# One layer on one Trainium2 core: where the first up weights are cast, and two buffers shared by three kinds of small tile

## The chip, the cores and the metric

The kernel runs on one core of one Trainium2 chip. Its time is device microseconds for one launch, from a comparison of several executions; lower is better. A core has a matrix engine (TensorE, PE in the profile, with its weight loads as PEld), VectorE (DVE), ScalarE (ACT), GpSimd (POOL), and SyncE (SP), which here issues nearly all DMA transfers. Each engine works through its own instructions strictly in order and waits on semaphores for the others.

## The reference, cut to what matters

One decoder layer over a sequence of 1024 rows and a width of 1024, all in float32:

```python
xn = rmsnorm(x, attn_norm_g)
proj = einsum('bsd,de->bse', xn, w_in)            # q, k, v of both head groups, forget gates
out_a = swa_sinks_attention(qa, ka, va, sinks)    # 8 heads, window of 128, ALiBi
out_b = forgetting_attention(qb, kb, vb, log_f)   # 8 heads, causal, bias c[t] - c[s]
x = x + einsum('bse,ed->bsd', concat(out_a, out_b), w_out)
hn = rmsnorm(x, mlp_norm_g)
hid = square(relu(einsum('bsd,df->bsf', hn, w_up)))     # 4096 wide
x = x + einsum('bsf,fd->bsd', hid, w_down)
```

q and k are normalised per head; `c` is the running sum of the logarithms of the forget gates.

## The kernel before, in words

**Split operands.** To keep float32 accuracy every matmul operand is split into a rounded part hi and a remainder lo = x - hi, and three products are summed (hi·hi, hi·lo, lo·hi). The helper `split` (L75) does this for weights: line L77 is the cast on ACT that writes hi, line L80 the subtraction, on POOL or DVE, that writes lo. So one pair of weights is one ACT cast, then one subtraction, and TensorE needs both. For the activations `h_split` (L975) does the same with the gain of the norm folded in: L977 is the cast on ACT, L978 the remainder on DVE.

**Order of the work.** The code is traced as it stands; the framework then orders the instructions of each engine by a simulated timeline, with priorities that follow the traced order. `tc.high_priority` lifts a block in it, and `with tc.issue_after(ins):` forces every instruction traced in the block that runs on the engine of `ins` to be issued after `ins`. The order on each engine is fixed at build time. Buffers are named by tags: tiles of one tag take turns in its `bufs` places, and the first writer of a new tile waits until the last user of the place is done.

**Attention.** TensorE projects q, k, v for a pair of heads (`proj`) while the heads before are scored. In the forgetting heads (`scores_b`, L672) a block of 128 queries is scored against up to 1024 keys in pieces of 512 columns (`spb`). For the piece on the diagonal POOL first copies the broadcast decay row with the future masked out (`cm`, L694), then one DVE instruction adds it to the scores and takes the row minimum (L699), ACT takes the exponential (L704), and for the last pair of heads DVE or POOL normalises (L711, L713, L715). TensorE transposes the probabilities (`tpb`, L740), ACT and DVE split them (`pth` L402, `ptl` L403), and TensorE multiplies by v (`pvb`). The norms of q and k (`qknorm`, L266) square a block on POOL into a tile `sq` (L279) that DVE then sums (L284). The gates (`forget_gates`, L466) work in a tile `zt`. Before the change `sq` and `zt` share one place of 512 columns, and `cm` has one place of its own, of the same size.

**Output projection.** `w_out` is taken in 8 columns blocks `dt`, the first four row tiles of each during attention (`out_first`, the sums go to memory as `part_d`), the other four at the end: dt = 0 and 4 beside the last attention units, then dt = 1, 5, 2, 6, 3, 7. `out_weights` (L869) loads and splits the weights into a place given by the list `WOS`. `out_finish` (L982) loads `part_d` into `h` (place w2 for dt < 4, w3 for 4 to 6, a tile `rr` for dt = 7), adds the sums of TensorE (L988), stores h to memory (`h_d`, L989), and splits h for the next stage. For dt < 4 this is `h_split` of the left half (product 1), and the cast `b12` (L994) of the right half into place w4; for dt > 3 it is `h_split` of both halves (products 2 and 3) and three DVE sums `ts` (L1007), which are split as well (`sum_splits`, products 5, 6, 7 and 4).

**Up projection.** The 4096 columns are made 2 x 128 at a time (index j of 16) by seven products, a Strassen-Winograd scheme, in the order `UP = (1, 2, 3, 6, 7, 5, 4)`. One product is 12 matmuls over four row tiles k: hi·hi, hi·lo, lo·hi for each k. The split activations `bh[n]`, `bl[n]` stay in place for all j; the row tile k = 3 of each comes from dt = 3 and dt = 7, the last to be finished. `up_weights` (L1048) takes the next of seven weight places from `w_slot` (L1044) and splits; lo is written by DVE for n in (2, 6, 5) and by POOL for 1, 3, 7, 4. For j = 0 and j = 1 the weights of product 1 are split ahead (`up_ahead`), and TensorE runs product 1 for both before product 2. The weight places w0 to w6 are shared with `h`, `b12` and the weights of the output projection, which is why their rotation matters here.

**Down projection.** Seven products again, in four phases; the page's lines `pd`, `hx` and `wx` belong to it. The change does not touch it.

Of the kernel before, what the change touches and what calls it, by code (L numbers as in the profile page):

```python
# [8 lines left out]
F32 = mybir.dt.float32  # L9
# [7 lines left out]
P = 128  # L17
# [38 lines left out]
def hybrid_layer(  # L56
# [209 lines left out]
    def qknorm(x, nh, tlo, thi, r=None):  # L266


        n = thi - tlo
        w = nh * HD  # L270
        ss, r0, u = (
            ap3.tile([P, 16], F32, tag=tag, name=tag, bufs=2)[:, : n * nh]
            for tag in ("ss", "sr0", "su")
        )
        m = n // 2
        for i in range(2):
            sq = ap2.tile([P, 512], F32, tag="sq", name="sq", bufs=1)[:, : m * w]
            xv = x[:, tlo + i * m : tlo + (i + 1) * m, :w]
            square = nc.gpsimd.tensor_tensor(  # L279
                out=sq.rearrange("p (t c) -> p t c", t=m), in0=xv, in1=xv, op=ALU.mult  # L280
            )
            if i == 0:
                squared.append(square.ins)
            nc.vector.tensor_reduce(  # L284
                out=ss[:, i * m * nh : (i + 1) * m * nh],
                in_=sq.rearrange("p (g d) -> p g d", d=HD), axis=AX.X, op=ALU.add,
            )
        th = lambda a: a.rearrange("p (t h) -> p t h", h=nh)
        nc.vector.scalar_tensor_tensor(
            out=th(ss), in0=th(ss), scalar=1.0 / HD,  # L290
            in1=ep2[:, tlo:thi].unsqueeze(2).to_broadcast([P, n, nh]),
            op0=ALU.mult, op1=ALU.add,
        )
        nc.scalar.activation(r0, ss, AF.Ln)
        nc.scalar.activation(r0, r0, AF.Exp, scale=-0.5)
        nc.vector.tensor_tensor(out=u, in0=r0, in1=r0, op=ALU.mult)
        nc.vector.tensor_tensor(out=u, in0=u, in1=ss, op=ALU.mult)
        na = nh + (2 if r is not None else 0)
        if r is None:
            rv = ap3.tile([P, 16], F32, tag="r", name="r", bufs=2)[:, : n * nh]  # L300
            rv = th(rv)
        else:
            rv = r[:, tlo:thi, :]
        nc.vector.scalar_tensor_tensor(
            out=rv[:, :, :nh], in0=th(u), scalar=3.0, in1=th(r0),
            op0=ALU.subtract, op1=ALU.mult,
        )
        for t in range(n):
            xt = x[:, tlo + t, : na * HD].rearrange("p (h d) -> p h d", d=HD)
            nc.gpsimd.tensor_tensor(  # L310
                out=xt, in0=xt, in1=rv[:, t].unsqueeze(2).to_broadcast([P, na, HD]), op=ALU.mult
            )
# [153 lines left out]
    def forget_gates():  # L466
        nc.vector.tensor_tensor(
            out=z, in0=z, in1=bfb.unsqueeze(2).to_broadcast([P, NH, NT]), op=ALU.add
        )
        zf = z.rearrange("p h t -> p (h t)")  # L470

        zt = ap2.tile([P, 4, NT * NH], F32, tag="sq", name="zt", bufs=1)
        ze, zs, zp = zt[:, 0], zt[:, 1], zt[:, 2]
        nc.vector.scalar_tensor_tensor(out=ze, in0=zf, scalar=-1.0, in1=zf, op0=ALU.mult, op1=ALU.min)
        nc.scalar.activation(ze, ze, AF.Exp)
        nc.vector.tensor_scalar(out=zs, in0=ze, scalar1=2.0, scalar2=None, op0=ALU.add)
        nc.vector.reciprocal(zs, zs)
        nc.vector.tensor_tensor(out=zs, in0=zs, in1=ze, op=ALU.mult)
        nc.vector.tensor_tensor(out=ze, in0=zs, in1=zs, op=ALU.mult)
        nc.vector.tensor_scalar_mul(zp, ze, 2.0 / 17.0)  # L480
        for n in (15, 13, 11, 9, 7, 5, 3):
            nc.vector.scalar_tensor_tensor(
                out=zp, in0=zp, scalar=2.0 / n, in1=ze, op0=ALU.add, op1=ALU.mult
            )
        nc.vector.scalar_tensor_tensor(out=zp, in0=zp, scalar=2.0, in1=zs, op0=ALU.add, op1=ALU.mult)
        nc.vector.scalar_tensor_tensor(
            out=zt[:, 3], in0=zf, scalar=0.0, in1=zp,
            op0=ALU.min, op1=ALU.subtract,
        )
        pt = pa.tile([P, 512], F32, tag="tr", name="ptf", bufs=3)  # L490
        nc.tensor.transpose(pt[: NH * NT, :P], zt[:, 3], ident)
        cum = ap2.tile([P, 256], F32, tag="mt", name="cum", bufs=2)[: NH * NT, :P]
        nc.vector.tensor_tensor_scan(
            out=cum, data0=ones1[: NH * NT].to_broadcast([NH * NT, P]),
            data1=pt[: NH * NT, :P], initial=0.0, op0=ALU.mult, op1=ALU.add,
        )
        off = pa.tile([P, 512], F32, tag="tr", name="off", bufs=3)
        mm(
            off[: NH * NT, 0:1], before.rearrange("p h t -> p (h t)"),
            cum[:, P - 1 : P], True, True,  # L500
        )
        offs = ap3.tile([NH * NT, 1], F32, name="offs")
        nc.vector.tensor_copy(offs, off[: NH * NT, 0:1])
        nc.vector.tensor_scalar(
            out=cum, in0=cum, scalar1=offs[:, 0:1], scalar2=None, op0=ALU.add
        )
        nc.sync.dma_start(c_d.rearrange("h (t q) -> (h t) q", q=P), cum)
# [164 lines left out]
    def scores_b(p, qp, h):  # L672
        q1, k1, k2, cb = heads[p, "q"][h], heads[p, "k1", h], k2_of[h], heads[p, "cb", h]
        probs = []
        for i in (2 * qp, 2 * qp + 1):
# [8 lines left out]
            for c in range((nk + 511) // 512):  # L684
                n = min(512, nk - c * 512)
                ne = max(n, 256)
                ks = slice(c * 512, c * 512 + ne)
                sp = pa.tile([P, 512], F32, tag="sc", name="spb", bufs=2)
                mm(sp[:, :ne], qs, k1[:, ks], True, False)
                pe = mm(sp[:, :ne], qs, k2[:, ks], False, True)  # L690
                bias = cb[:, c * 512 : c * 512 + n]
                if (c + 1) * 512 >= nk:
                    cm = ap2.tile([P, 512], F32, tag="cm", name="cm", bufs=1)[:, :n]
                    nc.gpsimd.affine_select(  # L694
                        out=cm, in_=bias, pattern=[[-1, n]], compare_op=ALU.is_ge,
                        fill=BIG, base=n - P, channel_multiplier=1,
                    )
                    bias = cm
                nc.vector.tensor_tensor_reduce(  # L699
                    out=pr[:, c * 512 : c * 512 + n], in0=sp[:, :n], in1=bias, scale=1.0,  # L700
                    scalar=3e38 if c == 0 else nm[:, 0:1],
                    op0=ALU.add, op1=ALU.min, accum_out=nm[:, c : c + 1],
                )
# [159 lines left out]
        mix_tiles(e)  # L863
        return nc.sync.dma_start(mixt[e].bitcast(F32), mixs_d[e].rearrange("c p s -> p c s"))

    WOS = ("w5", "w6", "w0", "w1", "w5", "w6")
    nout = [0]

    def out_weights(dt, e0):  # L869
        i = nout[0] = nout[0] + 1  # L870
        wr = o["zw"].tile([P, 4, P], F32, tag="wor", name="wor", bufs=2)
        nc.sync.dma_start(wr, w_o[dt][:, e0 : e0 + 4, :])
        w = slot(WOS[i - 11] if i > 10 else f"w{i % 2}", "wos", [2, 4, P], F32R)
        split(w[:, 0], w[:, 1], wr, nc.scalar, nc.gpsimd)
        return w[:, 0], w[:, 1]

# [97 lines left out]

    def h_split(n, t, src, gain):  # L975
        hi, lo = bh[n][:, t, :], bl[n][:, t, :]
        nc.scalar.activation(hi, src, AF.Copy, scale=gain)  # L977
        nc.vector.scalar_tensor_tensor(  # L978
            out=lo, in0=src, scalar=gain, in1=hi.bitcast(F32), op0=ALU.mult, op1=ALU.subtract
        )  # L980

    def out_finish(dt, ps):  # L982
# [7 lines left out]
        if dt < 4:  # L990
            h_split(1, t, h[:, left], gain)
            ts = part["t"] = slot("r1", "ts", [4, 512])
            b12 = part["b12"] = slot("w4", "b12", [512])
            nc.scalar.activation(b12, h[:, right], AF.Copy, scale=gain)  # L994
            nc.vector.scalar_tensor_tensor(
                out=ts[:, 0], in0=h[:, left], scalar=gain, in1=b12, op0=ALU.mult, op1=ALU.subtract
            )
            return
# [44 lines left out]

    def w_slot(name, shape, dt=F32):  # L1044
        nw[0] += 1
        return slot(f"w{(0, 1, 5, 6, 2, 3, 4)[(nw[0] - 1) % NW]}", name, shape, dt)

    def up_weights(n, src):  # L1048
        w = w_slot("wu", [2, 4, P], F32R)
# [14 lines left out]
    def bank(name):  # L1064
        nbank[0] += 1
        return pm.tile([P, 512], F32, tag=f"m{nbank[0] % 8}", name=name, bufs=1)

    for dt in (1, 5, 2, 6, 3, 7):
        w = out_weights(dt, 4)
        ps = [bank(f"po{c}") for c in range(2)]  # L1070
# [2 lines left out]
        if dt == 5:  # L1073
            with tc.issue_after(part["load"].ins):
                up_load(1)
        if dt == 3:
            up_ahead = [up_weights(1, up_sums[0][1]), up_weights(1, raws[1][:, 0, :4])]

# [13 lines left out]
    def up(j):  # L1092
# [4 lines left out]
        for n in UP:  # L1097
            if n == 1 and j == 1:
                m[n] = second.pop()
            else:  # L1100
                w = up_ahead.pop(0) if n == 1 and j == 0 else up_weights(n, src[n])
                m[n] = bank(f"pu{n}")
                up_products(n, w, m[n])
            if n == 1 and j == 0:
# [299 lines left out]
```

## Time and profile before

| | |
|---|---|
| median of 3 executions | 1088.91 us (1088.8 to 1089.02) |
| the profiled execution: time, span of its instructions | 1092.64 us, 1090.9 us |
| granted TensorE clock, mean | 0.997 |
| TensorE busy | 1074.9 us (99% of the span) |
| DVE, ACT, POOL busy | 773.2, 577.0, 388.8 us |
| attention with projections | to about 431 us |
| rest of the output projection | 431 to 469 us |
| up projection | 469 to 782 us |
| down projection | 782 us to the end |

A row of the timeline gives start and duration in microseconds, engine, line, operation, out<-in, shapes and count, and in brackets the idle time of the engine before it with what ended it. A row of stretches gives for each engine its busy time and, in parentheses, its instructions, then the granted clock of TensorE (1.00 is full speed), the busy share of the DMA engines and GB/s. A row of waits gives total, times and the longest. PE's busy time counts a matmul as busy whether it runs at full clock or at half.

### The profile page before, as it was taken

The page shows a single profiled execution, that of the slowest core. Times are in us where ns is not written, and L with a number is a line of the kernel's source. Part 1 is how long each engine was busy: PE and PEld are TensorE (multiplying, and loading weights), DVE is VectorE, ACT ScalarE, POOL GpSimd, SP SyncE. Part 2 cuts the span into 40 slices and gives each one's busy share as a digit, 9 for nine tenths or more (in the row PEclk, how much of TensorE's full clock was granted, in tenths as well). Part 3 has the DMA queues.
Part 4 walks back from the last instruction along what each step waited for, and adds up shares of the span by engine and source line. Part 5 has one row for each costly group of instructions (what it writes and reads, how often), then busy time and mean ns, then how long its engine had stood idle before and what let it go on. Part 6 is the DMA issues. An engine that isn't in the chain of part 4 may idle for free.

```text
span 1090.9 us, 15569 instructions
## 1 busy us (share of the span) xinstructions
PE 1074.9 (99%) x5492; PEld 933.1 (86%) x5492; DVE 773.2 (71%) x1319; ACT 577.0 (53%) x1022; POOL 388.8 (36%) x350
## 2 busy tenths in 40 slices
PE   9999999999999999989999999999999999999998
PEld 8999999999998887868888888888888888888886
DVE  7377787877866787887776759665675876664395
ACT  5558587776867765545545453443533433333331
POOL 4572433547456653233332232332222232131100
PEclk9999999999999999999999999999999999999999
DMA  8401112334747664643545443443998895665523
GB/s 281 168 19 57 62 46 62 116 99 128 253 155 248 230 196 169 220 172 142 193 167 202 174 164 117 147 172 145 331 390 311 308 327 190 218 234 185 176 88 115
DMA packets 96222, 195.67 MB, mean 179 GB/s; under 512 B 7392, under 2 KB 19856, under 8 KB 96144
## 3 DMA queue, kind: packets, MB, share of 16 engines
q1 hardware_dynamic: 95856, 194.54, 51.6%
q8 instruction: 43, 0.70, 0.3%
q14 instruction: 35, 0.29, 0.1%
q10 hardware_dynamic: 288, 0.15, 0.0%
HBM read 141.61 MB, written 53.04 MB: 178 GB/s over the span
## 4 chain that ended last, share of the span: by engine, by line
PE 67%; DVE 4%; DMA 3%; issue 1%; ACT 1%; SPq 0%; DVEq 0%; ACTq 0%
PE pu L73 28%; PE pd L73 28%; PE po L73 4%; PE pvb L73 2%; PE tpb L740 2%; PE spb L73 1%; DMA mix_d<-mtb 1%; PE ps L73 1%; DMA h<-part_d 1%; DMA h_d<-h 1%; DVE h L988 1%; DVE bl L978 0%; DVE ptl L403 0%; DVE ts L1007 0%; DMA mixn<-rd_d 0%
## 5 line engine op out<-in xcount | busy, mean ns | idle before, releaser
L73 PE MATMUL pd<-hx,wx 128*128 128x512 f32 (+1 forms) x1350 | 304.9, 388 | 0.0
L73 PEld LDWEIGHTS pd<-hx,wx 128*128 128x128 f32 x1350 | 252.7, 188 | 52.2
L73 PE MATMUL pu<-bh,wu 128*128 128x512 f32 x896 | 277.9, 391 | 3.6 <-ACT bh L977 3.6
L73 PEld LDWEIGHTS pu<-bh,wu 128*128 128x128 f32 x896 | 169.0, 189 | 39.4 <-ACT bh L977 4.0
L73 PE MATMUL ps<-w,x 128*128 128x384 f32 (+1 forms) x960 | 196.5, 342 | 1.1 <-POOL w L80 0.8
L73 PE MATMUL pu<-bl,wu 128*128 128x512 f32 x448 | 175.2, 391 | 0.2 <-DVE bl L978 0.2
L73 PEld LDWEIGHTS ps<-w,x 128*128 128x128 f32 x960 | 165.1, 188 | 5.3 <-POOL w L80 1.5
L77 ACT CAST hx<-hr 128x1024 fp32r<-128x1024 f32 x56 | 59.0, 1054 | 174.9 <-PE pd L73 170.6
L80 POOL TENSOR_TENSOR wx<-wda,wx 128x1024 fp32r<-128x1024 f32 x24 | 66.1, 2755 | 194.8 <-ACT wx L77 172.4
L80 DVE TENSOR_TENSOR hx<-hr,hx 128x1024 fp32r<-128x1024 f32 x56 | 77.4, 1387 | 75.7 <-ACT hx L77 75.7
L73 PEld LDWEIGHTS pu<-bl,wu 128*128 128x128 f32 x448 | 84.5, 189 | 18.3 <-DVE bl L978 0.7
L80 POOL TENSOR_TENSOR wu<-wus,wu 128x512 fp32r<-128x512 f32 x32 | 48.0, 1502 | 130.5 <-ACT wu L77 130.5
L73 PE MATMUL po<-mix,wos 128*128 128x512 f32 x384 | 93.4, 393 | 0.0
L73 PEld LDWEIGHTS po<-mix,wos 128*128 128x128 f32 x384 | 70.7, 188 | 14.0 <-ACT pc L916 0.2
L77 ACT CAST wu<-wus 128x512 fp32r<-128x512 f32 x64 | 39.3, 620 | 80.7 <-PE pu L73 73.2
L80 POOL TENSOR_TENSOR wu<-wur,wu 128x512 fp32r<-128x512 f32 x32 | 47.0, 1469 | 86.5 <-ACT wu L77 86.5
L1027 DVE TENSOR_TENSOR ht<-hb 128x512 f32<-128x512 f32 x32 | 22.9, 757 | 64.1 <-ACT hb L1131 64.1
L704 ACT ACTIVATE sb<-sb,nmb 128x128 f32<-128x128 f32 (+3 forms) x64 | 49.8, 779 | 26.8 <-DVE nmb L699 26.1
L403 DVE TENSOR_TENSOR ptl<-tpb,pth 128x512 fp32r<-128x512 f32 (+1 forms) x80 | 50.1, 631 | 18.3 <-ACT pth L402 17.9
L77 ACT CAST wx<-wda 128x1024 fp32r<-128x1024 f32 x56 | 58.5, 1049 | 8.1 <-DMA wda<-in_w_d_dram 8.1
L80 POOL TENSOR_TENSOR w<-wr,w 128x384 fp32r<-128x384 f32 (+1 forms) x47 | 49.9, 1069 | 29.6 <-ACT w L77 15.8
L694 POOL TENSOR_SCALAR_AFFINE_SELECT cm<-cb 128x128 f32<-128x128 f32 (+1 forms) x64 | 30.8, 482 | 60.2 <-DVE nmb L699 59.6
(205 smaller groups left out, 1829.9 us busy)
## 6 DMA issues: line engine op xcount, KB each, us to landing
wda<-in_w_d_dram SPq DMA_DIRECT2D x34, 1024.0 KB, 9.2
hr<-hid_d SPq DMA_DIRECT2D x56, 512.0 KB, 5.8
wur<-in_w_u_dram SPq DMA_DIRECT2D x32, 512.0 KB, 4.4
hid_d<-ht SPq DMA_DIRECT2D x16, 1024.0 KB, 4.4
hid_d<-hb SPq DMA_DIRECT2D x16, 768.0 KB, 3.9
mix<-mixs_d SPq DMA_DIRECT2D x7, 1024.0 KB, 5.7
wr<-in_w_b_dram SPq DMA_DIRECT2D x32, 192.0 KB, 2.5
xq<-in_x_dram SPq DMA_DIRECT2D x8, 512.0 KB, 5.8
```

The lines of the kernel that those rows point to most:

```text
L73: return nc.tensor.matmul(out, lhsT, rhs, start=start, stop=stop)
L77: hi_eng.copy(hi, src)
L80: return lo_eng.tensor_tensor(out=lo, in0=src, in1=hi.bitcast(F32), op=ALU.subtract)
L403: nc.vector.tensor_tensor(out=lo[:, cols], in0=pt[:, cols], in1=hi[:, cols].bitcast(F32), op=ALU.subtract)
L694: nc.gpsimd.affine_select(out=cm, in_=bias, pattern=[[-1, n]], compare_op=ALU.is_ge, fill=BIG, base=n - P, channel_multiplier=1,)
L704: nc.scalar.activation(pr[:, :nk], pr[:, :nk], AF.Exp, scale=-1.0, bias=nm[:, c : c + 1], accum_out=dn_b[p % 2][:, h, i : i + 1] if p < 3 ...
L740: nc.tensor.transpose(tp[:, c0 : c0 + P], probs[qi][:, kb * P : (kb + 1) * P], ident)
L988: nc.vector.tensor_tensor(out=h[:, cs], in0=ps[c], in1=h[:, cs], op=ALU.add)
L1027: eng.tensor_tensor(out=out, in0=a, in1=b, op=ALU.subtract)
```

## The change

**Casts.** `out_finish` now remembers its latest L977 or L994 cast in `part["cast"]`, and the loop over dt = 1, 5, 2, 6, 3, 7 collects them: `casts[-2]` is the b12 cast of dt = 3, `casts[-1]` the last L977 cast of dt = 7. In `up(0)` the ACT casts of the weights of product 2 are issued behind `casts[-2]`, those of products 3, 6, 7, 5, 4 behind `casts[-1]`.

**Places.** The rotation of the weight places and the list `WOS` are changed to go with it. For j = 0 the products 1 (j = 0), 1 (j = 1), 2, 3, 6, 7, 5, 4 took w0, w1, w5, w6, w2, w3, w4, w0; now they take w1, w5, w0, w6, w3, w4, w2, w1. In the output projection's second half dt = 0, 4, 1, 5, 2, 6, 3, 7 took w1, w0, w5, w6, w0, w1, w5, w6; now w1, w5, w0, w6, w1, w5, w0, w6.

**Small tiles.** `sq`, `zt` and `cm` now share one tag with two places; the memory is the same as before.

```diff
@@ qknorm
-            sq = ap2.tile([P, 512], F32, tag="sq", name="sq", bufs=1)[:, : m * w]
+            sq = ap2.tile([P, 512], F32, tag="sq", name="sq", bufs=2)[:, : m * w]
@@ forget_gates
-        zt = ap2.tile([P, 4, NT * NH], F32, tag="sq", name="zt", bufs=1)
+        zt = ap2.tile([P, 4, NT * NH], F32, tag="sq", name="zt", bufs=2)
@@ scores_b
-                    cm = ap2.tile([P, 512], F32, tag="cm", name="cm", bufs=1)[:, :n]
+                    cm = ap2.tile([P, 512], F32, tag="sq", name="cm", bufs=2)[:, :n]
@@ out_weights
-    WOS = ("w5", "w6", "w0", "w1", "w5", "w6")
+    WOS = ("w5", "w0", "w6", "w1", "w5", "w0", "w6")
...
-        w = slot(WOS[i - 11] if i > 10 else f"w{i % 2}", "wos", [2, 4, P], F32R)
+        w = slot(WOS[i - 10] if i > 9 else f"w{i % 2}", "wos", [2, 4, P], F32R)
@@ h_split, out_finish
-        nc.scalar.activation(hi, src, AF.Copy, scale=gain)
+        part["cast"] = nc.scalar.activation(hi, src, AF.Copy, scale=gain)
...
-            nc.scalar.activation(b12, h[:, right], AF.Copy, scale=gain)
+            part["cast"] = nc.scalar.activation(b12, h[:, right], AF.Copy, scale=gain)
@@ w_slot
-        return slot(f"w{(0, 1, 5, 6, 2, 3, 4)[(nw[0] - 1) % NW]}", name, shape, dt)
+        return slot(f"w{(1, 5, 0, 6, 3, 4, 2)[(nw[0] - 1) % NW]}", name, shape, dt)
@@ loop over dt
+    casts = []
...
+        casts.append(part["cast"].ins)
@@ up
-                w = up_ahead.pop(0) if n == 1 and j == 0 else up_weights(n, src[n])
+                with tc.issue_after(casts[-2 if n == 2 else -1]) if j == 0 else nullcontext():
+                    w = up_ahead.pop(0) if n == 1 and j == 0 else up_weights(n, src[n])
```

## The prediction, made before the changed kernel was built

> **What bounds the kernel now.** I read the page's busy times first, then TensorE's own waits, then the stretches around them, and last the timelines of the engines in those stretches.
>
> ```profile
> PE 1074.9 (99%) x5492; PEld 933.1 (86%) x5492; DVE 773.2 (71%) x1319; ACT 577.0 (53%) x1022; POOL 388.8 (36%) x350
> ```
>
> TensorE has work for 1074.9 of 1090.9 us, and the change takes no matmul away. It can only win back TensorE's gaps, 16 us in all, and slow clock. Where these lie:
>
> ```profile
> 110.00:330.00 220.00, 218.44 (x1425) 208.44 (x1423) 164.57 (x420) 158.21 (x378) 105.56 (x129) 1.00 0.38 118
> 418.00:431.00 13.00, 10.31 (x62) 8.96 (x60) 8.80 (x18) 6.91 (x15) 0.94 (x1) 0.87 0.72 251
> 469.00:482.00 13.00, 9.21 (x33) 6.87 (x32) 10.89 (x17) 7.16 (x13) 2.56 (x2) 0.87 0.63 242
> 482.00:1082.00 600.00, 600.00 (x2645) 496.18 (x2644) 412.78 (x478) 254.87 (x287) 155.99 (x84) 1.00 0.57 203
> ```
>
> The 600 us of up and down projection behind 482 have no gap. Two places stand out, both of them also with a clock below 1: the end of attention (2.7 us idle) and the start of the up projection (3.8 us idle).
>
> ```profile
> PE pu L73 <- ACT bh L977: 3.6, 1, 3.6
> PE tpb L740 <- DVE ptl L403: 2.6, 1, 2.6
> PE ps L73 <- POOL w L80: 0.8, 1, 0.8
> ```
>
> Each place is one single wait. The clock behind each:
>
> ```profile
> 421.70:425.10 3.40, 3.40 (x19) 3.37 (x17) 1.55 (x4) 1.89 (x4) 0.00 (x0) 0.51 0.34 90
> 476.30:479.70 3.40, 3.38 (x8) 2.71 (x9) 3.32 (x5) 2.74 (x5) 1.29 (x1) 0.51 0.00 0
> 479.70:483.10 3.40, 3.40 (x16) 2.79 (x16) 3.40 (x6) 2.52 (x6) 0.56 (x1) 0.99 0.39 154
> ```
>
> After each long wait the clock is 0.51 for 3.4 us, so each wait costs 3.4 x 0.49 = 1.7 us more than the idle time shows: 8 matmuls where the next 3.4 us do 16. The 0.8 us wait for POOL lies in the attention's first part, whose clock stays at 1.00; a gap of that size does not bring the half clock.
>
> **The change at the start of the up projection.** What holds TensorE, on ACT, in the chain of waits and on PE:
>
> ```profile
> 473.09 0.62 ACT L77 CAST wu<-wus 128x512 fp32r<-128x512 f32 x1 [3.20 <-DMA h_d<-h]
> 473.62 0.61 ACT L77 CAST wu<-wur 128x512 fp32r<-128x512 f32 x1
> 474.14 0.72 ACT L977 ACTIVATE bh<-h,vt 128x512 fp32r<-128x512 f32 x1
> ...
> 466.57 6.42 DMA h_d<-h
> ...
> 430.96 38.33 PE L73 MATMUL po<-mix,wos 128*128 128x512 f32 x168
> 470.94 0.39 PE L73 MATMUL pu<-bh,wu 128*128 128x512 f32 x1
> 474.91 0.72 PE L73 MATMUL pu<-bh,wu 128*128 128x512 f32 x2 [3.58 <-ACT bh L977]
> 476.32 0.80 PE L73 MATMUL pu<-bl,wu 128*128 128x512 f32 x1 [0.22 <-DVE bl L978]
> ```
>
> The cast at 473.09 writes a weight place that held h of dt = 6: it waits for the store of h, issued at 466.57 and 6.42 us long. In order behind it stand the weights of product 2 and the L977 cast of dt = 3, the one TensorE lacks for k = 3 of product 1. The change orders both weight casts behind the casts of dt = 3 (and most behind those of dt = 7), so ACT has nothing in front of 474.14 that waits for a store. DVE's side:
>
> ```profile
> 470.35 1.29 DVE L988 TENSOR_TENSOR h<-po,h 128x512 f32<-128x512 f32 x2
> 471.55 0.69 DVE L80 TENSOR_TENSOR bl<-ts,bh 128x512 fp32r<-128x512 f32 x1
> 474.26 1.34 DVE L80 TENSOR_TENSOR wu<-wur,wu 128x512 fp32r<-128x512 f32 x1 [2.03 <-ACT wu L77]
> 475.52 0.74 DVE L978 SCALAR_TENSOR_TENSOR bl<-h,vt,bh 128x512 fp32r<-128x512 f32 x1
> 476.85 0.68 DVE L988 TENSOR_TENSOR rr<-po,rr 128x512 f32<-128x512 f32 x1
> 478.22 0.68 DVE L988 TENSOR_TENSOR rr<-po,rr 128x512 f32<-128x512 f32 x1
> ```
>
> The left half of h of dt = 3 is there at about 471.05 (half of the row at 470.35), the cast ends at 471.8 instead of 474.86. TensorE ran dry at 470.94 + 0.39 = 471.33, so 0.45 us of the 3.58 stay, and the 0.22 for bl with it. Without the long gap the half clock goes too. Removed: 3.58 + 0.22 + 1.7 = 5.5; left: 0.7.
>
> What is late next. A matmul takes 38.33 / 168 = 0.228 us. From 471.8 the 15 left of the two products 1 end at 475.4 and product 2 at 478.1; product 3 wants its lo weights as third matmul, at 478.6. These come after dt = 7's last cast. DVE now goes on at 472.2 and does bl, one ts, the weights of product 2, rr left, one bl, rr right: six steps at the 0.6 to 0.7 between the starts above, so rr is done at about 476.0 instead of 478.9. One L977 cast (0.72), the weights' cast (0.62) and POOL's subtraction (1.3, the shorter rows below) end at about 478.6, on the spot. If POOL has to wait for one DVE instruction first, 0.6 is lost, and DVE in turn stands still for the subtraction, which may cost product 6 another 0.3. Product 6 takes the place of h of dt = 6, stored at 473; product 7 that of b12, read last by DVE at about 477; product 5 that of h of dt = 3, stored at the latest 6.4 us after 471.7; all these precede their casts, which follow 476.7. Sum: -5.5 + 0.7 + 0.9 = **-3.9**. The bounds: -4.8 if POOL is never late, and on the other side the case of the next rows.
>
> ```profile
> 482.54 6.09 POOL L80 TENSOR_TENSOR wu<-wur,wu 128x512 fp32r<-128x512 f32 x1 [3.08 <-ACT wu L77]
> ...
> 560.38 1.85 POOL L80 TENSOR_TENSOR wu<-wus,wu 128x512 fp32r<-128x512 f32 x1 [2.87 <-ACT wu L77]
> ...
> 478.18 1.29 POOL L80 TENSOR_TENSOR wu<-wus,wu 128x512 fp32r<-128x512 f32 x1 [3.12 <-ACT wu L77]
> ...
> 487.40 0.68 DVE L1030 TENSOR_TENSOR hb<-pu,u 128x512 f32<-128x512 f32 x1
> 488.00 1.18 DVE L1030 TENSOR_TENSOR wus<-wur 128x512 f32<-128x512 f32 x1
> ...
> 560.99 1.78 DVE L1030 TENSOR_TENSOR ht<-hb,ht 128x512 f32<-128x512 f32 x1
> ```
>
> The same subtraction takes 1.29 us when it starts with DVE's add of rr (478.22, which reads PSUM). At 560.38 it waits 0.6 for one DVE instruction, and the next DVE instruction, 560.99, then takes 1.78. But the one at 482.54, in the very stretch of the change, ends only 1.23 us after DVE's `hb<-pu` at 487.40 began, an instruction that reads PSUM: it got nothing while DVE went from one instruction on SBUF to the next. The Trainium skill ("SBUF — State Buffer", section "SBUF: two separate sides") says that a port pair shared by the two goes to whichever starts first, for its whole instruction, while the other blocks. Read as a wait of one DVE instruction that rule keeps the sum at -3.9; the row at 560.38 agrees with it, the row at 482.54 does not, and by that row the sum is the +4.2 of the slower rival.
>
> The new rotation of `WOS` costs nothing by itself: every place of the second half of the output projection now has its last user four blocks back (24 matmuls each, 5.5 us), before it was three to four, and TensorE has no gap between 431 and 469, where its 168 matmuls hide it; without that cover it would be one cast of 0.62.
>
> **The change in attention.** Two places let POOL make the next `cm` while DVE still has the last one. It makes none of the 64 faster. TensorE is filled with projections there, except at the end:
>
> ```profile
> 412.86 2.53 POOL L917 TENSOR_TENSOR xt<-xt,pc 128x512 f32<-128x512 f32 x2 [0.52 <-ACT pc L916]
> 415.35 0.85 POOL L694 TENSOR_SCALAR_AFFINE_SELECT cm<-cb 128x256 f32<-128x256 f32 x1
> ...
> 413.22 0.34 DVE L699 CUSTOM_DVE_ANT_0 sb<-spb,cm,nmb 128x128 f32<-128x128 f32 x1
> 414.56 1.39 DVE L624 TENSOR_TENSOR mixr<-mixr,mixn 128x512 f32<-128x512 f32 x1
> 417.67 0.47 DVE L699 CUSTOM_DVE_ANT_0 sb<-spb,cm,nmb 128x256 f32<-128x256 f32 x1
> ...
> 413.97 0.28 PE L73 MATMUL spb<-k2z,q1b 128*128 128x256 f32 x1
> 420.81 1.27 PE L740 MATMUL tpb<-ident,sb 128*128 128x128 f32 x7 [2.56 <-DVE ptl L403]
> ...
> 418.18 0.94 ACT L704 ACTIVATE sb<-sb,nmb 128x768 f32<-128x768 f32 x1 [1.59 <-DVE nmb L699]
> ```
>
> The last scores are ready at 414.25. Their `cm` could not start before DVE had read the last one (413.56), and POOL was by then in two additions until 415.39. So DVE's 417.67 is ordered behind other work, the exponential starts at 418.18, and TensorE waits until 420.81. With a second place POOL can make this `cm` before the additions, and DVE can take the scores between 414.3 and, behind the L624 multiply, 415.95: the chain moves up by 1.7 to 3.4 us. I take 1.7, the nearer row: 0.9 of the gap then stays, about the 0.8 that left the clock alone, so the half clock (1.7) goes too: -3.4. The bounds are 0 (the order stays) and -4.3 (all of 2.6 + 1.7). From this I take back 0.7: TensorE at full speed meets the last chain of ACT and DVE steps, which the half clock between 421.7 and 425.1 now covers, and I give it one such step. The other 60 copies, the 28 squares and the gates get a new order on POOL and DVE. In 110 to 330 TensorE now loses 1.6 us; half as much again, 0.8, is my price for that, between 0 and another 1.6. Sum: **-1.9**.
>
> **Total:** -3.9 - 1.9 = -5.8 against the profiled execution's 1092.64, of which 1090.9 is span. The median without a profile is 3.7 lower, and I take the gaps to be the same there: 1088.9 - 5.8 = **1083.1 us**.
>
> **The rivals.**
> - *Up start only* (the order at the end of attention stays, with some loss from the new order): -3.9 + 0.8, 1085.8. For it: order is drawn at build time, and nothing says DVE's slot is moved. Against it: the row at 417.67 follows its `cm` by 1.5 us only because other work was placed between.
> - *No change that can be told.* POOL misses two or three DVE instructions (1.2 to 1.8), product 3 waits, the half clock returns: -5.5 + 0.7 + 1.8 + 1.7 = -1.3, and attention gives 0 to -1: 1086.7 to 1088. What counts as no change is 0.2%, 2.2 us, about what a measurement can tell. It would also come out so if the changed code did not do what it says, that is if ACT's order at 473 had another store to wait for.
> - *Slower: POOL shut out.* Product 3's subtraction now starts at about 477.3, 1.3 us after the add of rr, in the middle of DVE's SBUF instructions, where before it met the add itself (478.18). If it gets in only with `hb<-pu`, which came 487.40 - 478.22 = 9.2 us after the add of rr began, it starts at 475.4 + 9.2 = 484.6 and ends at 485.9: 7.3 us after TensorE wants it, plus 1.7 of half clock: -5.5 + 0.7 + 7.3 + 1.7 = +4.2, with nothing from attention 1093.1. It decides from a wait of 3.1 us on: below that the place still gains. For it stands the row at 482.54, against it the one at 560.38 and the shape of DVE's row after it.
>
> **How the numbers follow.** Both places gain: 0.44, own range 1080 to 1085. Up start only: 0.19. No change: 0.21, of which 0.02 faster. Slower: 0.16. So faster 0.65, same 0.19, slower 0.16. The range has to hold 8 in 10: from 1079.6 (-4.8 - 4.3 = -9.1, all bounds at their best, is 1079.8) to 1091.8, which leaves out most of the slower case.
>
> **What would show it.** Right: on ACT the L977 cast of dt = 3 within 1 us of its add, no clock below 0.9 between 465 and 490, TensorE's wait for `bh` under 0.6; the L699 of 256 columns less than 2.5 us after its scores; the wait of `tpb` under 1 us. Wrong: a wait `pu <- POOL wu` of several us, an L80 row of POOL longer than 2 us at the start of the up projection, or new waits of TensorE between 110 and 415 that sum to over 3 us.

## The result, and the profile after

The changed kernel takes 1093.62 us (median, 1091.79 to 1096.44), the kernel before in the same comparison 1089.85 us (1087.27 to 1093.64). The ratio is 1.0035, 95% interval 1.0028 to 1.0043: **slower, by about 3.8 us**. The prediction was 1083.1 us, range 1079.6 to 1091.8; the time lies outside it and on the other side. The profiled execution of the changed kernel takes 1095.26 us, its span is 1093.6. Both profiled executions are longer than their medians: by 1.6 us here, and by 2.8 us before (1092.64 against 1089.85).

TensorE's busy time hardly moves, so the loss is again in gaps and clock. First the line of busy times of the changed kernel:

```profile
PE 1076.0 (98%) x5492; PEld 934.1 (85%) x5492; DVE 779.0 (71%) x1319; ACT 575.1 (53%) x1022; POOL 384.7 (35%) x350
```

Where the time went is read from three milestones: the last scores of the forgetting heads (`spb`), the first product of the up projection (`pu`) and the first sum for the norm that is taken during the up projection (`pms`). These are lines of the views by tile; "a to b" is the first and the last start. Before:

```profile
L73 PE MATMUL spb<-k2z,q1b x96: 278/389/480, 180.6 to 414.0; 128*128 128x512 f32 x48, 128*128 128x256 f32 x32, 128*128 128x384 f32 x16
...
L73 PE MATMUL pu<-bh,wu x896: 388/389/793, 469.1 to 781.3; 128*128 128x512 f32 x180
...
L73 PE MATMUL pms<-rr,ones x4: 590/592/592, 665.5 to 666.8; 128*128 128x512 f32 x4
```

And after:

```profile
L73 PE MATMUL spb<-k2z,q1b x96: 274/389/628, 178.8 to 423.2; 128*128 128x512 f32 x48, 128*128 128x256 f32 x32, 128*128 128x384 f32 x16
...
L73 PE MATMUL pu<-bh,wu x896: 388/389/793, 475.8 to 783.9; 128*128 128x512 f32 x180
...
L73 PE MATMUL pms<-rr,ones x4: 590/592/592, 668.1 to 669.4; 128*128 128x512 f32 x4
```

The span grows by 1093.6 - 1090.9 = 2.7 us, in four stretches. Up to the last scores the changed kernel loses 423.2 - 414.0 = **9.2**. From there to the first `pu` it takes 52.6 instead of 55.1: **-2.5**. From `pu` to `pms` 192.3 instead of 196.4: **-4.1**. The rest takes 425.5 instead of 425.4. So in these two profiles both places that the change is about came out close to the forecast (-2.7 and -3.9), and the middle of attention lost more than both gained.

The stretches of the changed kernel (columns as in the prediction):

```profile
110.00:330.00 220.00, 214.06 (x1390) 203.73 (x1389) 156.60 (x400) 152.81 (x365) 102.51 (x122) 1.00 0.36 115
330.00:418.00 88.00, 86.60 (x497) 75.26 (x498) 62.39 (x158) 60.67 (x129) 53.83 (x60) 0.96 0.57 199
418.00:431.00 13.00, 11.79 (x81) 10.23 (x80) 10.79 (x29) 9.59 (x24) 8.59 (x9) 1.00 0.71 231
469.00:482.00 13.00, 12.39 (x54) 9.82 (x53) 12.18 (x20) 7.29 (x12) 1.30 (x1) 1.00 0.69 254
482.00:1082.00 600.00, 599.50 (x2641) 495.19 (x2640) 422.58 (x483) 255.95 (x294) 153.09 (x86) 1.00 0.56 204
```

The one of them that the prediction did not show, before:

```profile
330.00:418.00 88.00, 88.00 (x526) 76.41 (x524) 64.14 (x156) 61.31 (x132) 57.61 (x62) 1.00 0.64 213
```

Between 110 and 330 TensorE is now idle 5.9 us instead of 1.6, between 330 and 418 1.4 instead of 0, and there the clock is 0.96, worth 88 x 0.04 = 3.5 us. Together 4.4 + 1.4 + 3.5 = 9.3, the 9.2 of the milestones. The waits of the changed kernel (total, times, longest) say who is late. The last line shown, on POOL, is one that the kernel before does not have:

```profile
PE spb L73 <- DVE nmb L699: 3.1, 4, 1.0
PE tpb L740 <- DVE ptl L403: 2.8, 2, 1.5
...
POOL cm L694 <- DVE nmb L699: 26.8, 20, 3.3
POOL sq L279 <- DVE nmb L699: 16.8, 4, 7.2
```

The scores wait for L699, that is for DVE's step that reads `cm`. And POOL's squares stand 16.8 us behind copies that hold both shared places and that DVE has not read yet:

```profile
179.97 1.04 POOL L279 TENSOR_TENSOR sq<-qkb 128x512 f32<-128x512 f32 x1 [7.18 <-DVE nmb L699]
```

That was the first suspect. It turned out not to be the cause.

### The profile page after: what moved, and what is told of

Its sections match the earlier page's. It is cut to its first block, busy times and chain, and to the rows that moved or that the text cites. A ratio compares the mean times of both kernels' runs of the same rounds, so it can differ in the third digit from the quotient of the medians.

```text
span 1093.6 us, 15570 instructions
## 1 busy us (share of the span) xinstructions
PE 1076.0 (98%) x5492; PEld 934.1 (85%) x5492; DVE 779.0 (71%) x1319; ACT 575.1 (53%) x1022; POOL 384.7 (35%) x350
## 4 chain that ended last, share of the span: by engine, by line
PE 90%; DVE 4%; DMA 2%; issue 2%; ACT 1%; POOL 1%; SPq 0%; POOLq 0%; DVEq 0%; ACTq 0%
PE pd L73 27%; PE pu L73 27%; PE ps L73 14%; PE po L73 7%; PE pvb L73 3%; PE spb L73 3%; PE tpb L740 3%; PE sp L73 1%; PE pv L73 1%; PE tpa L565 1%; DMA xq<-in_x_dram 1%; DMA wr<-in_w_a_dram 1%; PE ptk L331 1%; PE ptq L331 1%; DVE x L207 0%
## 5 line engine op out<-in xcount | busy, mean ns | idle before, releaser
L73 PE MATMUL ps<-w,x 128*128 128x384 f32 (+1 forms) x960 | 194.2, 342 | 2.5 <-ACT z L460 1.4
L80 POOL TENSOR_TENSOR wx<-wda,wx 128x1024 fp32r<-128x1024 f32 x24 | 65.8, 2740 | 195.2 <-ACT wx L77 195.2
L80 DVE TENSOR_TENSOR hx<-hr,hx 128x1024 fp32r<-128x1024 f32 x56 | 72.5, 1303 | 71.8 <-ACT hx L77 71.8
L80 POOL TENSOR_TENSOR wu<-wus,wu 128x512 fp32r<-128x512 f32 x32 | 46.6, 1458 | 127.7 <-ACT wu L77 127.7
L80 POOL TENSOR_TENSOR wu<-wur,wu 128x512 fp32r<-128x512 f32 x32 | 43.5, 1360 | 89.8 <-ACT wu L77 89.8
L80 POOL TENSOR_TENSOR w<-wr,w 128x384 fp32r<-128x384 f32 (+1 forms) x47 | 49.9, 1073 | 39.8 <-ACT w L77 29.1
L740 PE MATMUL tpb<-ident,sb 128*128 128x128 f32 x288 | 47.1, 277 | 4.0 <-DVE ptl L403 2.8
```

What stands on the lines that cost most here:

```text
L73: return nc.tensor.matmul(out, lhsT, rhs, start=start, stop=stop)
L80: return lo_eng.tensor_tensor(out=lo, in0=src, in1=hi.bitcast(F32), op=ALU.subtract)
L740: nc.tensor.transpose(tp[:, c0 : c0 + P], probs[qi][:, kb * P : (kb + 1) * P], ident)
```

## The experiments

All ratios are to the kernel before, run beside it on the same chip. The groups ran on different chips, so kernels of different groups are compared by their ratios; a step of 0.001 is 1.09 us. The **up start** is everything in the diff but its three tile lines. Three theories for the loss:

- **A, held places.** Copies that wait for DVE hold both shared places, and the squares stand behind them.
- **B, any new order.** The order of 60 copies was redrawn, and any redrawn order loses.
- **C, the tie** (formed after the second group). Places of one tag are handed out in the order in which the program writes its tiles. Sharing them ties copies and squares to that order, however many places there are.

### First group: which edit, and how much sharing

The up start alone (the three tile lines as before):

```diff
-            sq = ap2.tile([P, 512], F32, tag="sq", name="sq", bufs=2)[:, : m * w]
+            sq = ap2.tile([P, 512], F32, tag="sq", name="sq", bufs=1)[:, : m * w]
-        zt = ap2.tile([P, 4, NT * NH], F32, tag="sq", name="zt", bufs=2)
+        zt = ap2.tile([P, 4, NT * NH], F32, tag="sq", name="zt", bufs=1)
-                    cm = ap2.tile([P, 512], F32, tag="sq", name="cm", bufs=2)[:, :n]
+                    cm = ap2.tile([P, 512], F32, tag="cm", name="cm", bufs=1)[:, :n]
```

> Only the casts and the places of the weights are changed; sq, zt and cm are as before. In the changed kernel the stretch from the first matmul of the up projection to the mean square's takes 192.3 us against 196.4 before. Theory 1 (the two parts do not touch each other, and the small tiles alone cost the loss): about -4 us against before, 1085 to 1087; TensorE's first up matmul within 1 us of before (469.1), the clock at 1.00 behind it. Rival (the gain at the up projection only exists because the attention before it was late and DVE less far behind): -1 us or nothing, a wait of TensorE for bh or wu of over 2 us comes back.

Measured: 1086.96 us, ratio 0.9975 (0.9963 to 0.9988): -2.7 us, less than the forecast 4. No wait of over 2 us for `bh` or `wu` came back (0.9 us is the longest), so the rival falls. The first `pu` starts at 466.4, 2.7 us earlier than before and not within 1 us of it.

The three tile lines alone, with the up start as before:

> Only sq, zt and cm share two places; casts and weights as before. Theory 1: about +7 to +8 us against before, 1096 to 1098: attention ends 6.7 us late as in the changed kernel, and the wait at the up projection with its half clock stays. Rival (the parts interact): under +4.

Measured: 1098.77 us, ratio 1.0079 (1.0065 to 1.0092): +8.6 us, somewhat above the forecast. The two add up to +5.9 where the change as a whole gives +3.8, so they are not quite independent, but the signs are plain: the up start gains, the shared tiles lose.

The up start, and copies of odd blocks of queries put into the squares' place, one place each:

```diff
-                    cm = ap2.tile([P, 512], F32, tag="cm", name="cm", bufs=1)[:, :n]
+                    cm = ap2.tile([P, 512], F32, tag="sq" if i % 2 else "cm", name="cm", bufs=1)[:, :n]
```

> As the kernel with the casts alone, and for all pairs of heads cm takes the place of cm (even blocks) and that of sq (odd blocks) by turns, while sq and zt have only their own place. Theory A: sq competes with every second copy, POOL stands before sq while an odd copy is held: a loss against the casts alone of at least 3 us, with a wait of sq for DVE's nmb in POOL's waits of over 5 us in total. Theory B: the loss does not go with that wait; the time may lie within 2 us of the casts alone or over 5 us above.

Measured: 1089.3 us, ratio 0.9992 (0.9983 to 1.0001), 1.9 us above the up start. POOL's squares wait 8.3 us for `nmb`, half of the 16.8. That is the wait that A expected, but not the loss of at least 3 us.

The same, but only in the last pair of heads (`p == 3 and i % 2`):

> As the kernel with the casts alone, and in the last pair of heads only, cm takes the place of cm and the idle place of sq by turns; for the pairs before, sq, zt and cm have one place each as before. Theory A (the loss comes from cm and sq competing for places while both are in use): no loss here, and the end of attention loses its wait: -6 to -8 us against before. Theory B (any other use of places redraws the order on POOL and DVE, and the drawn order costs the time): anything between -5 and +4, with TensorE's waits at new spots in the attention.

Measured: **1084.78 us**, ratio 0.9958 (0.9946 to 0.9971), 1.9 us below the up start though the intervals overlap; no square waits for `nmb`. The gain on the kernel before, 4.6 us by the ratio, is less than A's 6 to 8 and lies in the range that B allowed. So a second place for copies may be worth having, and sharing it seems to cost where squares are still to come. Up to here A fits in its order if not in its sizes: 0, 8.3 and 16.8 us of waiting squares go with no loss, a small one and a large one.

### Second group: a place more

To make room for a third place of 512 columns (2 KB), these kernels give up one of the three places of `ptl`. The control is the up start with two `ptl` places:

```diff
-        lo = ap2.tile([P, 512], F32R, tag="ptl", name="ptl", bufs=3)
+        lo = ap2.tile([P, 512], F32R, tag="ptl", name="ptl", bufs=2)
```

> The up start of the change with the attention's small tiles as before, but two places instead of three for the low halves of the transposed scores (ptl). It frees 2 KB for the next kernels and is their control. Expected by both theories: the same as with three places within 1.5 us, 1085.5 to 1088.5 us, and no wait of a square (L279) on POOL for nmb. Above 1090 the third ptl place matters itself, and the next kernels are to be read against this time only.

Measured: 1094.65 us, ratio 1.0042 (1.0029 to 1.0054). Both theories missed: the third `ptl` place is worth 0.0067, 7.3 us. The next two are read against this control.

Two own places for the copies, one for the squares:

```diff
-                    cm = ap2.tile([P, 512], F32, tag="cm", name="cm", bufs=1)[:, :n]
+                    cm = ap2.tile([P, 512], F32, tag="cm", name="cm", bufs=2)[:, :n]
```

> As the control with two ptl places, and the masked copies get two places of their own, the squares and the gates' tile keep one of their own: the doubling without the sharing. Theory A (the loss is POOL's squares standing behind copies that hold both places): no wait of a square for nmb, the loss is gone, the control's time within 2 us or better. Theory B (any redrawn order of the 60 copies in mid-attention loses): 4 to 9 us above the control although no square waits for nmb.

Measured: 1088.52 us, ratio 0.9989 (0.998 to 0.9998): 5.8 us better than the control. The copies' order is redrawn here too, and it gains: B falls in its wide form.

The shared ring with three places (`bufs=3` for `sq`, `zt` and `cm`, two for `ptl`):

> The changed kernel with a third place in the shared ring and two ptl places. Theory A: the wait of squares for nmb falls from 16.8 us to under 5 and the time to within 2.5 us of the control, about 1087 to 1089. Theory B (the order of POOL and DVE itself is bad wherever copies and squares take turns): it stays at 1092 or above, with TensorE's waits for nmb L699 and ptl L403 in mid-attention still there.

Measured: 1094.22 us, ratio 1.0041 (1.0029 to 1.0053), as the control and 5.7 us worse than two own places, with the same memory. The waits of POOL and PE in this kernel:

```profile
PE spb L73 <- DVE nmb L699: 3.2, 4, 1.5
...
POOL cm L694 <- DVE nmb L699: 22.9, 13, 5.1
POOL sq L279 <- ACT qkb L647: 57.4, 13, 14.3
```

No square waits for `nmb` any more, and TensorE still waits for `nmb` as much as in the changed kernel. **A falls here**: the held places were a symptom.

The changed kernel with each square ordered behind the latest copy written before it:

```diff
+            with tc.issue_after(copies[-1]) if copies else nullcontext():
                 square = nc.gpsimd.tensor_tensor(
```

> The changed kernel, two shared places, and each square is issued behind the latest masked copy written before it in the program, so no copy can be queued behind a later square that waits for its projection tile. If the loss comes from copies queued behind squares (first seen at 193 us, where the square waits for ACT's qkb): TensorE's waits spb<-nmb go and the time falls to 1087 to 1089. If it comes from squares queued behind copies that hold both places (16.8 us of square waits): those waits stay or grow and the time stays at 1092 or above.

Measured: 1093.19 us, ratio 1.0035 (1.0023 to 1.0048), the changed kernel again, with 16.9 us of waiting squares. By the words of the expectation this would speak for squares behind held places. But the edit does not change POOL's order at all: that order was already there, so the run tests neither side. That gave C. In the changed kernel and in the ring of three POOL's 64 copies and 28 squares come in exactly the order in which the program writes them. The first `cm` shows it, in the view by tile, before and after:

```profile
L694 POOL TENSOR_SCALAR_AFFINE_SELECT cm<-cb x64: 286/505/1006, 134.1 to 415.3; 128x128 f32<-128x128 f32 x16, 128x256 f32<-128x256 f32 x16, 128x384 f32<-128x384 f32 x16, 128x512 f32<-128x512 f32 x16
```

```profile
L694 POOL TENSOR_SCALAR_AFFINE_SELECT cm<-cb x64: 288/502/1086, 163.1 to 421.2; 128x128 f32<-128x128 f32 x16, 128x256 f32<-128x256 f32 x16, 128x384 f32<-128x384 f32 x16, 128x512 f32<-128x512 f32 x16
```

At 134.1 the squares of the next pair of heads were still to come; now the first copy has to follow two of them.

### Third group: the order without the sharing

The up start, every tile in its own place as before the change, and POOL in written order by force:

```diff
+            with tc.issue_after(copies[-1]) if copies else nullcontext():
                 square = nc.gpsimd.tensor_tensor(
...
+                    with tc.issue_after(squares[-1]):
-                    nc.gpsimd.affine_select(
+                        copy = nc.gpsimd.affine_select(
```

> The up start of the change, every tile in a place of its own as before (one for the copies, one for the squares and the gates' tile, three for ptl), but POOL issues squares and copies in the order in which the program writes them: each copy behind the latest square written before it, each square behind the latest copy written before it. That is the order that the changed kernel and the ring of three have on POOL. Theory C (a shared ring hands its places out in the order of writing and so ties two streams together; that order is what costs): as the changed kernel without its second place, 1092 to 1096, first pu product at 474 or later. Theory A (places held by copies that nobody reads yet): the places are as before, so no more than 2 us above the change's up start alone, 1086 to 1089.

Measured: 1095.97 us, ratio 1.0053 (1.0034 to 1.0071), 0.0078 or **8.5 us above the up start** (0.9975), with no place shared and no square waiting for `nmb`. POOL's copies and squares come in the order of the changed kernel. The first `pu` starts at 473.1 in its profile, which is a short execution (1093.38 us); the expectation had 474 or later.

One half of it: copies behind squares, squares free.

> As the run in written order, with one half of the tie alone: each copy behind the latest square written before it; the squares are free. Theory C has two halves: copies held back by squares that wait for their projection tile, or squares (and so the norms and the next pair of heads) held back by copies that wait for DVE. If the first half costs, this is 1091 or above; if the second, it is at 1086 to 1089 with the up start alone. Theory A: 1086 to 1089.

Measured: 1095.28 us, ratio 1.0048 (1.0031 to 1.0065): 8.0 us above the up start.

The other half: squares behind copies, copies free.

> The other half of the tie alone: each square behind the latest copy written before it; the copies are free, every tile in its own place as before, with the up start of the change. Theory C1 (what costs is copies held behind squares that wait for their projection tile): as the up start alone, 1086 to 1089. Theory C2 (both directions cost): 1091 or above.

Measured: 1084.84 us, ratio 0.9964 (0.9949 to 0.9978): 1.2 us below the up start, within its interval. So the whole cost is in **copies held behind squares**; C1 holds.

Two own places for the copies and two of `ptl`, as in the second group, in written order:

> Two own places for the copies, one for the squares, two for ptl (1088.52 us with a free order), and POOL issues squares and copies in the written order. Theory C: as the shared ring of three, which has the same order, 1092 to 1096. Theory A (places): within 2 us of 1088.5.

Measured: 1093.85 us, ratio 1.0042 (1.0024 to 1.0059). The order alone takes two own places from 0.9989 to 1.0042, 5.8 us; the ring of three, with the same order, gave 1.0041. That accounts for what the ring of three lost.

How the tie delays TensorE shows where the second block of keys is scored. The up start alone: POOL's timeline, then DVE's, then TensorE's, in 6 us.

```profile
188.54 0.40 POOL L694 TENSOR_SCALAR_AFFINE_SELECT cm<-cb 128x256 f32<-128x256 f32 x1 [0.86 <-DVE nmb L699]
191.46 1.04 POOL L279 TENSOR_TENSOR sq<-qkb 128x512 f32<-128x512 f32 x1 [2.52 <-ACT qkb L647]
...
188.10 0.35 DVE L699 CUSTOM_DVE_ANT_0 sb<-spb,cm,nmb 128x128 f32<-128x128 f32 x1
192.15 0.48 DVE L699 CUSTOM_DVE_ANT_0 sb<-spb,cm,nmb 128x256 f32<-128x256 f32 x1 [0.52 <-PE spb L73]
...
193.44 0.48 PE L73 MATMUL spb<-k1b,q1b 128*128 128x512 f32 x1
```

The same with own places in written order (the added lines of code shift L279, L694 and L699 to L280, L697 and L703):

```profile
190.50 1.04 POOL L280 TENSOR_TENSOR sq<-qkb 128x512 f32<-128x512 f32 x1 [3.57 <-ACT qkb L649]
191.50 0.29 POOL L697 TENSOR_SCALAR_AFFINE_SELECT cm<-cb 128x128 f32<-128x128 f32 x1
194.66 0.40 POOL L697 TENSOR_SCALAR_AFFINE_SELECT cm<-cb 128x256 f32<-128x256 f32 x1
...
192.18 0.34 DVE L703 CUSTOM_DVE_ANT_0 sb<-spb,cm,nmb 128x128 f32<-128x128 f32 x1
195.55 0.47 DVE L703 CUSTOM_DVE_ANT_0 sb<-spb,cm,nmb 128x256 f32<-128x256 f32 x1
...
196.09 0.50 PE L73 MATMUL spb<-k1b,q1b 128*128 128x512 f32 x1
```

A square needs its projection tile: it waits 3.57 us for ACT's copy `qkb`. The copy of 128 columns needs only the decay row, whose load ends at about 176, and its place, which DVE has read to the end at 181.85. But it stands behind that square on POOL, which works in order. DVE's L699 of 128 columns comes at 192.18 instead of 188.10, that of 256 at 195.55 instead of 192.15, and the next scores of 512 columns start at 196.09 instead of 193.44. In the changed kernel the same square starts at 193.02 and the same copy at 194.02:

```profile
193.02 1.04 POOL L279 TENSOR_TENSOR sq<-qkb 128x512 f32<-128x512 f32 x1 [2.13 <-ACT qkb L647]
194.02 0.29 POOL L694 TENSOR_SCALAR_AFFINE_SELECT cm<-cb 128x128 f32<-128x128 f32 x1
...
195.11 0.44 PE L73 MATMUL spb<-k1b,q1b 128*128 128x384 f32 x1 [0.87 <-DVE nmb L699]
```

Two runs remain. The up start with turns between the copies' and the squares' place in the last three of the eight heads (`2 * p + h > 4 and i % 2`), where almost no square is left to be tied:

> The up start of the change, and copies take turns between their own place and that of the squares in the last three of the eight heads (before: the last two, 1084.78 us). Almost no square is left to be tied there. Theory C: the second place is worth something wherever no square follows, so 1082 to 1085. Theory A expects the same. Above 1087 would say that the sharing costs even there.

Measured: **1084.78 us**, ratio 0.9948 (0.9935 to 0.9961). It has the lowest ratio of all, about 5.7 us faster than before. It lies 2.9 us below the up start, clear of its interval; it cannot be told from the last two heads alone (0.9958), nor from the squares behind copies (0.9964), which have no second place.

And one half of the up start's edits, the issue order of the casts without the new places:

```diff
-    WOS = ("w5", "w0", "w6", "w1", "w5", "w0", "w6")
+    WOS = ("w5", "w6", "w0", "w1", "w5", "w6")
-        return slot(f"w{(1, 5, 0, 6, 3, 4, 2)[(nw[0] - 1) % NW]}", name, shape, dt)
+        return slot(f"w{(0, 1, 5, 6, 2, 3, 4)[(nw[0] - 1) % NW]}", name, shape, dt)
```

> One half of the up start's edits: the casts of the first up weights are issued behind the casts of h, the places of the weights (the order of w_slot and WOS) as before, and the small tiles as before. If the issue order carries the gain, as the prediction has it, 1085.5 to 1088.5, the same as both halves together (1086.96). If the new places are needed for it (another cast behind a store): 1089 to 1092, with a wait of ACT for the store of h at 470 to 490.

Measured: 1087.87 us, ratio 0.9978 (0.997 to 0.9987). The issue order carries the gain (both halves 0.9975); the new places add nothing that can be told.

**The account.** Up start 0.9975 - 1 = -2.7 us; the tie 1.0053 - 0.9975 = +8.5; a second place under the tie, 1.0035 - 1.0053 = -2.0 (a difference of two close ratios, not resolved by itself). The sum is +3.8, the change as measured; it must come out so, since each term starts at the kernel where the one before ends.

## Why the prediction was wrong

**The step that failed** is the one term of 0.8 us "for that", the new order of the other 60 copies, 28 squares and the gates, bounded by 0 and 1.6. In the profile that stretch lost 9.2 us, in the runs the tie costs 8.5. The price was taken from a row that has nothing to do with the edit, TensorE's present idle time between 110 and 330 and half as much again. And the sentence ahead of it, that two places let POOL make the next `cm` while DVE still has the last one, read the edit as a doubling. It is a doubling and a merger: the copies gave up a place of their own for turns in a ring with another stream. The text on the kernel said that tiles of one tag take turns; followed one step further, a copy's turn comes after the squares written before it, and the squares wait for projection tiles. That wait was in the trace of before, 44.6 us in all, and was not looked at:

```profile
POOL sq L279 <- ACT qkb L647: 44.6, 13, 13.6
```

None of the rivals had it: the slower one had POOL shut out at the up start, and its 1093.1 is close to the measured time for the wrong reason.

**The up start**, -3.9: right in mechanism, too large in size. In the profile of the change it is -4.1, in the runs -2.4 to -2.7. The cast of the row tile k = 3 no longer stands behind a store, and POOL is not shut out. ACT and POOL after:

```profile
477.07 0.72 ACT L977 ACTIVATE bh<-h,vt 128x512 fp32r<-128x512 f32 x1 [1.18 <-DVE h L988]
478.36 0.60 ACT L77 CAST wu<-wur 128x512 fp32r<-128x512 f32 x1
...
483.50 1.30 POOL L80 TENSOR_TENSOR wu<-wus,wu 128x512 fp32r<-128x512 f32 x1 [11.74 <-ACT wu L77]
486.20 1.63 POOL L80 TENSOR_TENSOR wu<-wur,wu 128x512 fp32r<-128x512 f32 x1 [1.39 <-ACT wu L77]
487.79 1.75 POOL L80 TENSOR_TENSOR wu<-wus,wu 128x512 fp32r<-128x512 f32 x1
```

The cast at 477.07 now waits only for DVE's add and the weights' cast follows it. TensorE's waits left there are 0.61 and 0.49 us, for `bl` and not for `bh`, 1.1 in place of the 0.7 in the sum, and the clock stays at 1.00. The 0.9 for a late POOL was not needed: TensorE has no wait for weights of POOL there. That the new rotation "costs nothing by itself" holds within what the runs can tell (0.9978 without it, 0.9975 with it).

**The end of attention**, -3.4 + 0.7 = -2.7: right in the profile, -2.5. The wait fell to less than half and the half clock went:

```profile
428.62 1.16 PE L740 MATMUL tpb<-ident,sb 128*128 128x128 f32 x7 [1.21 <-DVE ptl L403]
```

DVE's L699 of 256 columns comes 2.0 us after its scores instead of 3.4, and the wait is 1.35 us shorter where the forecast had 1.7. How much of it the second place did is less sure: with the up start alone that wait is 1.0 us too, with the issue order alone it is 2.6, and these two kernels take the same time within their intervals. The order there is redrawn by any edit. What the runs do show is that taking turns in the last three heads alone lies 2.9 us below the up start; whether the place or the redrawn order does it is not shown.

**The slower rival**, POOL shut out by DVE's port: it did not happen. The three L80 rows above take 1.30 to 1.75 us; the 6.09 of the row at 482.54 did not come back. The longest of them is 0.45 us above the shortest, which fits a wait within one DVE instruction (0.6 to 0.7 in the prediction's rows). That is how the prediction read the lock of the Trainium skill ("SBUF — State Buffer", section "SBUF: two separate sides"). DVE seems to have waited in its turn: its two subtractions of weights from 486.60 on took 3.49 us beside POOL's, where two subtractions took 1.29 at 475.14 in the same profile. Why the row at 482.54 took 6.09 before stays open.

**The tests named.** Of those "that would show it wrong" the third was met: new waits of TensorE between 110 and 415 of more than 3 us. It was listed as a sign and given no mechanism and no chance of its own. Of the signs of being right four were met and one was not: the wait of `tpb` is 1.21 us, not under 1.

**Two slips in the working** change nothing in the sum. Under the old rotation the last user of a place was three to five blocks back, not three to four (w1 went from dt = 0 to dt = 6). And the rival of no change comes to 1086.6 to 1087.6 by its own terms, not 1086.7 to 1088.

## What to carry to other kernels

Giving a tile a second place by merging two tags is two edits: it doubles the places, and it ties two streams to the order in which the program writes them. On an engine that works in order, ask of each pair what the first waits for: here copies that wait for nothing stood behind squares that wait for a projection. Look for the wait that the other stream has on that engine in the trace (44.6 us here). It is not a price, since the tie cost 8.5, but it shows what the first stream may come to stand behind, and the idle time of the bounding engine does not. Share places only where the other stream has ended, or nearly so, as in the last three heads here.

## What the runs showed of the hardware

TensorE's half clock does not need one long gap. In the changed kernel two gaps of 1.54 and 1.05 us end 2.1 us apart, with 1.1 us of work between them. Each is shorter than the 2.6 that stood before the half clock at the end of attention:

```profile
330.02 0.52 PE L740 MATMUL tpb<-ident,sb 128*128 128x128 f32 x3 [1.54 <-DVE ptl L403]
332.16 0.80 PE L73 MATMUL spb<-k1b,q1b 128*128 128x512 f32 x1 [1.05 <-DVE nmb L699]
```

The stretches of that place, 3.4 us each but the third:

```profile
330.00:333.40 3.40, 2.33 (x11) 1.73 (x12) 3.37 (x9) 1.98 (x6) 1.96 (x3) 0.68 1.03 411
333.40:336.80 3.40, 3.40 (x17) 3.40 (x17) 1.41 (x7) 2.05 (x4) 2.45 (x4) 0.50 0.43 146
336.80:340.00 3.20, 3.20 (x15) 2.63 (x14) 2.51 (x6) 1.94 (x4) 3.20 (x5) 0.80 0.26 92
340.00:343.40 3.40, 3.40 (x17) 2.80 (x16) 1.65 (x5) 1.68 (x4) 1.28 (x2) 1.00 0.39 147
```

The clock is lost for (0.32 + 0.50) x 3.4 + 0.20 x 3.2 = 3.4 us, twice the 1.7 behind each long gap of before: more than the 2.6 us of idle time itself. The single gaps of 1.21, 0.61 and 0.49 us quoted above left the clock at 1.00. So did one of 1.85 us in the run in written order (at 425.95) and one of 1.96 with the squares behind copies (at 340.44). The Trainium skill ("TensorE: Matmul & The Clock Gate", section "Part 1: The HAM clock gate (the "warmup" mystery)") gives the slow state after at least one idle window of about 3.4 us. Here 2.6 us of idle time were enough, in one piece before and in two pieces after, so the measurement differs from that if an idle window is one without any work.

Not expected either: the third place of `ptl` is worth 7.3 us in the up start. And one thing stays open, why the gains at the two places are smaller in the runs than in the profiles. A part of it may be that the profiled execution before is a long one, 2.8 us above the median. The profile of the up start alone, which is at its median, has 193.4 us from `pu` to `pms`, 3.0 less than before and not 4.1. The prediction took the gaps of the long execution to be there in the median too, and no run shows that.
